# Weights loaded piece by piece into six small tiles, and two output stores of the delta heads issued later

## The chip, the cores and the metric

The kernel runs on one core of one Trainium2 chip. The number that counts is the time of one execution in microseconds of device time, as a median of several runs. Each engine of the core (PE for matrix products, DVE, ACT and POOL for elementwise work, SP as the queue that issues most of the copies) works through its own list of instructions in order, and waits on semaphores for the others. DMA transfers run beside them.

## The reference, cut to what matters

One layer, 256 positions, width 2048, all in float32. A vector `c` gives scale, shift and gate; the normalised input `h` is multiplied by a wide weight matrix, the product is cut into the inputs of two branches, and both are merged and projected back:

```python
shift, scale, gate = jnp.split(jax.nn.silu(c) @ w_ada + b_ada, 3, axis=-1)
h = rms_norm(x, norm_pre_w) * (1.0 + scale[:, None]) + shift[:, None]
proj = h @ w_in                       # 2048 x 24,656 columns, all weights read once
...
o_a = gated_delta_rule(q_a, k_a, v_a, g_log, beta)        # 32 heads, in chunks
o_a = rms_norm(o_a, gdn_norm_w) * jax.nn.silu(gdn_z.astype(jnp.float32)).reshape(...)
y_a = o_a.reshape(b, s, GDN_V_WIDTH).astype(x.dtype) @ w_proj_gdn
...
h_b = mlstm_chunkwise(q_b, k_b, v_b, ml_i + mlstm_b_i, ml_f + mlstm_b_f)   # 8 heads
y_b = h_b.astype(x.dtype) @ w_proj_mlstm
merged = jax.nn.sigmoid(gate_a) * y_a + jax.nn.sigmoid(gate_b) * y_b
out = merged @ w_out
return x + gate[:, None] * rms_norm(out, norm_post_w)
```

Some 320 MB of weights (the copies into `raw` and `ar`) are read, each once, and each weight serves 256 positions.

## The kernel before, in words

**The weight stream.** All weights of the large products go through one object, `Stream`. Its work is a list of *pieces* of 1024 columns by 128 rows (512 KB). For each piece, `prep` makes two tiles out of the raw tile: `whi`, a rounded copy (ACT, L176), and `wlo`, the remainder (DVE, L180; in the first 230 us partly POOL). Then `use` issues the matrix products of the piece: `whi` against the high part of `h`, `wlo` against the high part, `whi` against the low part. There are four `whi` and four `wlo` tiles, so that a piece is prepared up to four pieces before it is used. The raw tiles are loaded by *unit*: a unit is two pieces, one tile of 128 x 2048 (1 MB), and there are three such tiles. The load of a unit is put on SP's list as soon as the last piece of the unit three before it has been prepared in the program (`_loads`, which asks `before["done"]`), and on the chip it waits for that piece's `wlo`.

**What runs beside it.** After each used piece the stream calls `side.step()`, which advances every side generator by one `yield`. These generators hold the delta-rule heads, the mLSTM heads, the convolutions and the merge. `wait(n)` in them means n pieces later. What a generator issues in its step is placed on the engines' lists at this point; on SP it stands behind the loads issued so far. So the order of every engine's list is fixed when the program is built.

**A period.** The delta heads come in eight periods of four heads, from about 320 us to 1000 us. A period has 24 pieces: eight for q and k (`add_proj_t`, names `pt`, L658 and L662), eight for v (`add_proj_n` with a pair of groups, `pn`, L247; each of its loads is two copies, L166, that interleave two groups) and eight for the output gate (`add_z`). The side work of a period that matters here, in its order on SP:

- `ud` (L900): 32 x 32 diagonal blocks of the scores to DRAM, four copies of 16 KB for each of two head pairs; `ug` (L909): four copies that read each block row back to several partitions, 128 KB each; from them DVE computes block inverses (L928 to L934)
- `xd` (L937) and `xcmp` (L941): the inverses to DRAM and back in another layout (four copies); ACT (L948) and DVE (L945, L950) put them into `x0` and `y0`, and PE uses them in `mp`, `mx`, `mq`, `mz` (`gdn_stage2`)
- `vd`, `v`, `cw` (L834, L843, L849): the convolution of v; ACT then applies silu and a scale to `rr` (L885, L889), and PE multiplies it in `pa` (L1039)
- `o_dr` (L1112): the period's finished heads, transposed into two tiles `oT` (L1110), stored to DRAM, 256 KB each; they are read back only by the projection at 1200 us

After the periods come the mLSTM heads (to about 1210 us), the two projections `py` and the output product `pw`. The third part of `w_ada` (the gate) is loaded by the same stream, one unit each, and summed on DVE (L1311, L1313).

Of the kernel before, what the change touches and what calls it, by code (L numbers as in the profile page):

```python
# [15 lines left out]
P = 128  # L16
# [47 lines left out]
class Stream:  # L64


    def __init__(self, load, side, ahead=3):
        self.side, self.ahead = side, ahead
        self.load = (load, "w", 3)
        self.units, self.items, self.rings = [], [], {}  # L70
        self.loaded = self.used = self.prepared = self.pending = 0

    def add(self, src, prep, use, pieces=2, after=None, on_load=None, load=None):
        load, ring, bufs = load or self.load
        r = self.rings.setdefault(ring, [])
        u = dict(src=src, prep=prep, use=use, after=after, on_load=on_load, load=load, done=False,
                 before=r[-bufs] if len(r) >= bufs else None)
        r.append(u)
        i = len(self.units)
        self.units.append(u)  # L80
        for h in range(pieces):
            self.items.append((i, h, h == pieces - 1))

    def _loads(self):

        while self.loaded < len(self.units):
            u = self.units[self.loaded]
            if u["before"] is not None and not u["before"]["done"]:
                return
            u["raw"] = u["load"](u["src"])  # L90
            if u["on_load"]:
                u["on_load"]()
            self.loaded += 1

    def run(self):
        self._loads()
        while self.used < len(self.items):
            while self.prepared < len(self.items) and self.pending <= self.ahead:
                i, h, last = self.items[self.prepared]
                u = self.units[i]  # L100
# [5 lines left out]
            i, h, last = self.items[self.used]  # L106
            u = self.units[i]
            self.used += 1
            if u["use"]:
                self.pending -= 1  # L110
                u["use"](h, *u["p", h])
            if last and u["after"]:
                u["after"]()
            if u["use"]:
                self.side.step()
# [3 lines left out]
def hybrid_layer_kernel(  # L119
# [38 lines left out]
        SP.dma_start(t, src)  # L158
        return t

    def load_w(src):
        raw = wp.tile([P, 2048], F32, name="raw", tag="raw", bufs=3)
        c = 0
        for i, s_ in enumerate(src if isinstance(src, tuple) else (src,)):
            if isinstance(src, tuple) and len(s_.shape) == 3:
                SP.dma_start(raw.rearrange("p (k g c) -> p k g c", k=4, g=2)[:, :, i], s_)  # L166
                continue
            dst = raw[:, c:c + s_.shape[1] * (s_.shape[2] if len(s_.shape) == 3 else 1)]
            c += dst.shape[1]
            if len(s_.shape) == 3:  # L170
                dst = dst.rearrange("p (k n) -> p k n", k=s_.shape[1])
            SP.dma_start(dst, s_)
        return raw

    def split(src, hi, lo, eng=None):
# [29 lines left out]
    def prep_w(h, raw, width=2048):  # L205
# [3 lines left out]
        if begin:  # L209
            begin.pop()(raw[:, 0:n], hi, lo)  # L210
            return hi, lo
        split_w(raw[:, h * 1024:h * 1024 + n], hi[:, 0:n], lo[:, 0:n])
        return hi, lo

    freed = [-1] * 4
# [10 lines left out]
    def gfree(t):  # L226
        freed[slots[1].pop(id(t))[0]] = side.t
# [69 lines left out]
    def ada_tile():  # L297
        return sp.tile([P, 2048], F32, name="ar", tag="ar", bufs=ADA_BUFS)

    def load_ada(src):  # L300
        raw = ada_tile()
        SP.dma_start(raw, src)
        return raw
# [653 lines left out]
    def gdn_stage2(zg, res, zr):  # L957
# [146 lines left out]
        for z in range(2):  # L1104
            for h in range(2):
                for blk in range(2):
                    T.transpose(pts[z][:, h * S + blk * P:h * S + (blk + 1) * P], ons[z][:, blk, h], ident)
        for z in range(2):
            oT = bp.tile([P, 2, S], F32, name="oT", tag="oT")
            A.activation(oT.rearrange("p h t -> p (h t)"), pts[z], AF.Copy, scale=late_c["gnw"][:, 0:1])  # L1110
            gfree(pts[z])
            SP.dma_start(o_dr[4 * zg + 2 * z:4 * zg + 2 * z + 2].rearrange("h d t -> d h t"), oT)  # L1112

    def period_tail(zg, ps, qs, res, zr):
# [182 lines left out]
    def add_gate_unit():  # L1297
# [6 lines left out]
        gate_at[0] += 1  # L1304

        def prep(h, raw):
            side.debt += 2.4
            for q in range(2):
                if i == 0:
                    gate_half.append(bp.tile([P, 1024], F32, name=f"gacc{q}", tag=("ug", "rr")[q], bufs=1 + q))  # L1310
                    V.tensor_scalar(gate_half[q], raw[:, q * 1024:(q + 1) * 1024], sil[:, 0:1], None, op0=ALU.mult)  # L1311
                else:
                    V.scalar_tensor_tensor(gate_half[q], raw[:, q * 1024:(q + 1) * 1024], sil[:, i:i + 1],  # L1313
                                           gate_half[q], op0=ALU.mult, op1=ALU.add)
            if i == KC - 1:
# [318 lines left out]
```

## Time and profile before

| | |
|---|---|
| median of 3 runs | 1574.93 us (1571.59 to 1575.77) |
| the profiled execution | 1578.37 us, of which 1576.6 us lie between its first and last instruction |
| PE busy | 1554.4 us (99%) |
| DVE, ACT, POOL busy | 1172.0, 971.1, 269.9 us |
| DMA | 397.49 MB, mean 252 GB/s, 73.2% of 16 engines' time |
| matrix products | 8256 |
| copies of weights on SP | 227 of 1 MB, 80 of 512 KB, 12 of other sizes |

Busy shares are averages over very different stages. PE is the engine that is nearly always at work, so what counts is when it is not: its idle time, what it waited for then, and the stretches in which its clock is granted at half. A timeline row has the start and the length in us, the engine, the line, the operation, `out<-in`, the shapes, and in square brackets how long the engine was idle before it and what ended that.

### The profile page before, as it was taken

The numbers are of one execution on the slowest core, as the hardware profiler recorded it, in microseconds if no ns is written. First come the engines' busy times: TensorE is split into PE (matmuls) and PEld (weight loads), VectorE is DVE, ScalarE is ACT, GpSimd is POOL, SyncE is SP. The second block draws the span as 40 slices with busy tenths as digits, with TensorE's granted clock in tenths as the row PEclk, the third lists the DMA queues.
The fourth block names the chain that finished last, engine by engine and source line by source line (L and its number), as shares of the span: only waits on it lengthen the run. The fifth ranks groups of instructions, "written<-read, shape, count | busy, mean of one in ns | idle before, by whom it ended". The sixth has DMA issues, their size and how long they took to land.

```text
span 1576.6 us, 22531 instructions
## 1 busy us (share of the span) xinstructions
PE 1554.4 (99%) x8256; PEld 1297.2 (82%) x8256; DVE 1172.0 (74%) x1781; ACT 971.1 (62%) x1638; POOL 269.9 (17%) x213
## 2 busy tenths in 40 slices
PE   8999999999999999999999999999999999999998
PEld 5888888888888888888888888888888888888886
DVE  6786556867798988898979797866768766756654
ACT  7754446767566767676768676666566554544443
POOL 6787761001010101010101010100000000100100
PEclk9999999999999999999999999999999999999999
DMA  9998785975767685868586857656879877766573
GB/s 377 404 386 325 270 294 185 295 242 197 247 221 238 197 263 183 256 193 257 180 246 197 235 194 234 212 200 233 295 260 332 321 270 297 283 238 236 216 270 107
DMA packets 185956, 397.49 MB, mean 252 GB/s; under 512 B 27595, under 2 KB 137825, under 8 KB 158325
## 3 DMA queue, kind: packets, MB, share of 16 engines
q1 hardware_dynamic: 185460, 395.44, 73.2%
q8 instruction: 65, 1.06, 0.3%
q10 hardware_dynamic: 290, 0.53, 0.1%
q14 instruction: 45, 0.37, 0.1%
q0 software_dynamic: 96, 0.09, 0.0%
HBM read 375.37 MB, written 20.64 MB: 251 GB/s over the span
## 4 chain that ended last, share of the span: by engine, by line
PE 61%; issue 14%; DMA 12%; ACT 6%; DVE 5%; POOL 1%; SPq 1%; DVEq 0%; ACTq 0%; POOLq 0%
PE pn L247 37%; PE py L247 8%; PE pt L658 7%; DMA raw<-in_dram 7%; PE pt L662 3%; DMA xcmp<-xd 2%; DVE wlo L180 2%; ACT whi L176 2%; POOL mg L1424 1%; DMA ud<-au 1%; DMA ar<-in_dram 1%; DVE au L816 1%; PE pa L1039 1%; SPq L909 1%; DMA xd<-xx 0%
## 5 line engine op out<-in xcount | busy, mean ns | idle before, releaser
L247 PE MATMUL pn<-whi,h 128*128 128x512 f32 x2304 | 729.1, 392 | 1.0 <-ACT part L493 0.5
L180 DVE TENSOR_TENSOR wlo<-raw,whi 128x1024 fp32r<-128x1024 f32 (+1 forms) x455 | 558.3, 1235 | 210.9 <-ACT whi L176 207.3
L176 ACT CAST whi<-raw 128x1024 fp32r<-128x1024 f32 x508 | 524.1, 1045 | 281.3 <-PE pn L247 155.3
L247 PEld LDWEIGHTS pn<-whi,h 128*128 128x128 f32 x2304 | 432.6, 188 | 91.1 <-ACT h L176 1.1
L247 PE MATMUL pn<-wlo,h 128*128 128x512 f32 x1152 | 448.6, 389 | 0.2 <-POOL wlo L180 0.2
L247 PEld LDWEIGHTS pn<-wlo,h 128*128 128x128 f32 x1152 | 216.5, 188 | 43.4 <-POOL wlo L180 0.8
L658 PE MATMUL pt<-h,whi 128*128 128x512 f32 x768 | 249.6, 407 | 0.0
L247 PE MATMUL py<-whi,y 128*128 128x512 f32 x768 | 239.9, 391 | 0.0
L662 PEld LDWEIGHTS pt<-h,wlo 128*128 128x128 f32 x768 | 146.8, 191 | 34.9
L247 PEld LDWEIGHTS py<-whi,y 128*128 128x128 f32 x768 | 144.2, 188 | 30.3 <-issue 0.6
L180 POOL TENSOR_TENSOR wlo<-raw,whi 128x1024 fp32r<-128x1024 f32 (+1 forms) x67 | 146.5, 2197 | 45.0 <-ACT whi L176 41.3
L662 PE MATMUL pt<-h,wlo 128*128 128x256 f32 x768 | 153.3, 281 | 0.0
L247 PE MATMUL py<-wlo,y 128*128 128x512 f32 x384 | 149.5, 389 | 0.0
L658 PEld LDWEIGHTS pt<-h,whi 128*128 128x128 f32 x768 | 120.3, 192 | 2.4
L747 POOL TENSOR_SCALAR_AFFINE_SELECT dd<-gb 128x256 f32<-128x256 f32 x40 | 36.7, 941 | 451.8 <-DMA gb<-rows 322.6
L176 ACT CAST y<-ya 128x512 fp32r<-128x512 f32 x48 | 29.9, 622 | 129.5 <-PE py L247 119.0
L491 DVE TENSOR_TENSOR part<-pn,part 128x512 f32<-128x512 f32 x112 | 73.7, 685 | 44.9 <-PE pn L247 44.7
L180 DVE TENSOR_TENSOR y<-ya,y 128x512 fp32r<-128x512 f32 x48 | 33.2, 691 | 75.4 <-ACT y L176 75.3
L247 PEld LDWEIGHTS py<-wlo,y 128*128 128x128 f32 x384 | 72.1, 188 | 14.9
L247 PE MATMUL pw<-whi,m 128*128 128x512 f32 x256 | 80.0, 391 | 0.0
L437 DVE SCALAR_TENSOR_TENSOR ar<-ar,csil 128x2048 f32<-128x2048 f32 x30 | 68.3, 2278 | 6.1 <-DMA ar<-in_dram 6.1
L928 DVE TENSOR_TENSOR tmp<-xx,ug 128x6 f32<-128x6 f32 (+15 forms) x128 | 65.4, 511 | 3.2
(272 smaller groups left out, 1475.0 us busy)
## 6 DMA issues: line engine op xcount, KB each, us to landing
raw<-in_dram SPq DMA_DIRECT2D x227, 1024.0 KB
raw<-in_dram SPq DMA_DIRECT2D x80, 512.0 KB
ar<-in_dram SPq DMA_DIRECT2D x31, 1024.0 KB
v<-vd SPq DMA_DIRECT2D x24, 512.0 KB
cw<-conv_dr SPq DMA_DIRECT2D x32, 256.0 KB
ya<-o_dr SPq DMA_DIRECT2D x32, 256.0 KB
gate_dr<-part SPq DMA_DIRECT2D x11, 512.0 KB
gb<-rows SPq DMA_DIRECT2D x20, 256.0 KB
```

Source lines behind the costliest of these rows:

```text
L176: A.copy(hi, src)
L180: eng.tensor_tensor(lo, src, hi.bitcast(F32), op=ALU.subtract)
L247: T.matmul(ps, l, r, start=start and i == 0, stop=stop and i == 2, skip_group_check=True)
L437: V.scalar_tensor_tensor(raw, raw, 1.0, csil, op0=ALU.mult, op1=ALU.mult, accum_out=ad[:, pt * KC + k:pt * KC + k + 1])
L491: V.tensor_tensor(part[g][:, b], ps[b], part[g][:, b], op=ALU.add)
L658: T.matmul(ps, hi[:, o:o + P], h2[:, k].rearrange("p a s -> p (a s)"), start=k == 0, stop=k == KC - 1, skip_group_check=True)
L662: T.matmul(ps[:, 0:S], lo[:, o:o + P], h_hi[:, k], start=False, stop=k == KC - 1, skip_group_check=True)
L747: G.affine_select(dd[:, :, blk * S:blk * S + P], gb[:, :, blk * P:(blk + 1) * P], pattern=[[0, 2], [1, P]], compare_op=ALU.is_ge, fill=-1e ...
L816: V.scalar_tensor_tensor(au[:, h, c0:c0 + 2 * n].rearrange("p (a b) -> p a b", a=2), ps_[:, 0:2 * n].rearrange("p (a b) -> p a b", a=2), c ...
L909: SP.dma_start(ug[32 * q:32 * q + 32], ud[q].rearrange("m j i -> m (j i)").unsqueeze(0).broadcast_to([4, 8, 1024]))
L928: V.tensor_tensor(tmp[:, 0:nq, 0:w, 0:n], xx[:, 0:nq, 0:n].unsqueeze(2).broadcast_to([P, nq, w, n]), ug[:, 0:n, i:i + w].rearrange("p k c ...
L1039: T.matmul(pa[:, c], x0[:, 2 * g], rr[:, 0, c], start=True, stop=True)
```

## The change

A piece, not a unit, becomes what is loaded. The raw tile is 128 x 1024 (512 KB), and there are six instead of three, so that the memory is the same. A load is put on SP's list when the piece six before it has been prepared. The copies of the v pairs become four of 256 KB per pair of pieces in place of two of 512 KB; the gate's units are two pieces now, with the same arithmetic. The lists of PE, DVE, ACT and POOL are the same as before, instruction by instruction; only SP's list differs. It has 942 copies in place of 700.

The second edit: in periods 0 to 6 the two stores of `oT` are issued two and four pieces later, one each, instead of together at once.

```diff
-        self.load = (load, "w", 3)
-        self.units, self.items, self.rings = [], [], {}
+        self.load = (load, "w", 6)
+        self.items, self.rings = [], {}
...
     def add(self, src, prep, use, pieces=2, after=None, on_load=None, load=None):
...
-        u = dict(src=src, prep=prep, use=use, after=after, on_load=on_load, load=load, done=False,
-                 before=r[-bufs] if len(r) >= bufs else None)
...
         for h in range(pieces):
-            self.items.append((i, h, h == pieces - 1))
+            u = dict(src=src, h=h, prep=prep, use=use, after=after if h == pieces - 1 else None,
+                     on_load=on_load if h == 0 else None, load=load, done=False,
+                     before=r[-bufs] if len(r) >= bufs else None)
+            r.append(u)
+            self.items.append(u)
...
-            u["raw"] = u["load"](u["src"])
+            u["raw"] = u["load"](u["src"], u["h"])
...
-                u["p", h] = u["prep"](h, u["raw"])
-                u["done"] = last
+                u["p"] = u["prep"](u["h"], u["raw"])
+                u["done"] = True
...
-    def load_w(src):
-        raw = wp.tile([P, 2048], F32, name="raw", tag="raw", bufs=3)
...
+    def load_w(src, h):
+        raw = wp.tile([P, 1024], F32, name="raw", tag="raw", bufs=6)
+        if not isinstance(src, tuple):
+            if len(src.shape) == 3:
+                k = 1024 // src.shape[2]
+                SP.dma_start(raw.rearrange("p (k n) -> p k n", k=k), src[:, h * k:(h + 1) * k])
+            else:
+                SP.dma_start(raw, src[:, h * 1024:(h + 1) * 1024])
+            return raw
+        if len(src[0].shape) == 3:
+            for i, s_ in enumerate(src):
+                SP.dma_start(raw.rearrange("p (k g c) -> p k g c", k=2, g=2)[:, :, i], s_[:, 2 * h:2 * h + 2])
+            return raw
...
+        oTs = []
         for z in range(2):
             oT = bp.tile([P, 2, S], F32, name="oT", tag="oT")
             A.activation(oT.rearrange("p h t -> p (h t)"), pts[z], AF.Copy, scale=late_c["gnw"][:, 0:1])
             gfree(pts[z])
+            oTs.append(oT)
+        for z, oT in enumerate(oTs):
+            if zg < 7:
+                yield from wait(2)
             SP.dma_start(o_dr[4 * zg + 2 * z:4 * zg + 2 * z + 2].rearrange("h d t -> d h t"), oT)
...
-        stream.add(w_ada[32 + i], prep, None, 1)
+        stream.add(w_ada[32 + i], prep, None)
```

Two places show how SP's list moves; both stand in every full period, and are shown for the same one (about 690 us to 725 us in the profile of before). `raw<-in_dram` is a load of weights; 128x8x256 is a unit of q and k, 128x4x256 from L164 a piece of it (before, the same shape from L166 is one of the two copies of a v unit), 128x2x256 one of the two copies of a v piece.

First, SP from the block stores `ud` to the read-back `xcmp`. Before:

```order
L900 DMA ud<-au 32x4x32 x4
L172 DMA raw<-in_dram 128x8x256
L937 DMA xd<-xx 128x8x32
L172 DMA raw<-in_dram 128x8x256
L843 DMA v_7377<-vd 128x2x512
L849 DMA cw<-conv_dr 128x2x256 x2
L900 DMA ud<-au 32x4x32 x4
L941 DMA xcmp<-xd 32x1x256 x4
```

and with the change:

```order
L906 DMA ud<-au 32x4x32 x4
L164 DMA raw<-in_dram 128x4x256 x3
L943 DMA xd<-xx 128x8x32
L164 DMA raw<-in_dram 128x4x256
L849 DMA v_7655<-vd 128x2x512
L164 DMA raw<-in_dram 128x4x256
L855 DMA cw<-conv_dr 128x2x256 x2
L906 DMA ud<-au 32x4x32 x4
L947 DMA xcmp<-xd 32x1x256 x4
```

Four pieces of q and k stood before `xcmp`, now five do: one more load stands ahead of `xd`, half of the next one behind it, and one more ahead of `cw`.

Second, SP directly behind that, from `xcmp` to the store `vd`. Before:

```order
L941 DMA xcmp<-xd 32x1x256 x4
L172 DMA raw<-in_dram 128x8x256
L1112 DMA o_dr<-oT 128x2x256 x2
L909 DMA ug<-ud 32x1x1024 x4
L172 DMA raw<-in_dram 128x8x256
L166 DMA raw<-in_dram 128x4x256 x4
L834 DMA vd<-rr 128x2x512
```

and with the change:

```order
L947 DMA xcmp<-xd 32x1x256 x4
L164 DMA raw<-in_dram 128x4x256 x2
L915 DMA ug<-ud 32x1x1024 x4
L164 DMA raw<-in_dram 128x4x256
L1123 DMA o_dr<-oT 128x2x256
L170 DMA raw<-in_dram 128x2x256 x4
L1123 DMA o_dr<-oT 128x2x256
L170 DMA raw<-in_dram 128x2x256 x4
L840 DMA vd<-rr 128x2x512
```

Before, pieces 7 and 8 of q and k were one load behind the two stores and the four copies `ug`. Now piece 7 stands ahead of `ug`, only piece 8 behind it, and the stores stand further down among the loads of v.

More of the change, by code (lines that the diff above doesn't have):

```diff
@@ L75, in add @@
         r = self.rings.setdefault(ring, [])
[L76 to L82 removed]
+        for h in range(pieces):
+            u = dict(src=src, h=h, prep=prep, use=use, after=after if h == pieces - 1 else None,
[3 more added lines that the diff above has]
+            self.items.append(u)
     def _loads(self):
[L86 to L87 removed]
+        while self.loaded < len(self.items):
+            u = self.items[self.loaded]
             if u["before"] is not None and not u["before"]["done"]:
                 return
[L90 removed]
+            u["raw"] = u["load"](u["src"], u["h"])
             if u["on_load"]:
@@ L98, in run @@
             while self.prepared < len(self.items) and self.pending <= self.ahead:
-                i, h, last = self.items[self.prepared]
-                u = self.units[i]
+                u = self.items[self.prepared]
                 self.pending += u["use"] is not None
-                u["p", h] = u["prep"](h, u["raw"])
-                u["done"] = last
+                u["p"] = u["prep"](u["h"], u["raw"])
+                u["done"] = True
                 self.prepared += 1
                 self._loads()
-            i, h, last = self.items[self.used]
-            u = self.units[i]
+            u = self.items[self.used]
             self.used += 1
@@ L110, in run @@
                 self.pending -= 1
-                u["use"](h, *u["p", h])
-            if last and u["after"]:
+                u["use"](u["h"], *u["p"])
+            if u["after"]:
                 u["after"]()
@@ L159, in const @@
         return t
-    def load_w(src):
-        raw = wp.tile([P, 2048], F32, name="raw", tag="raw", bufs=3)
[L163 to L172, printed above, removed]
+    def load_w(src, h):
[11 more added lines that the diff above has]
+            return raw
+        c = -h * 1024
+        for s_ in src:
+            n = s_.shape[1]
+            a, b = max(0, -c), min(n, 1024 - c)
+            if a < b:
+                SP.dma_start(raw[:, c + a:c + b], s_[:, a:b])
+            c += n
         return raw
@@ L211, in prep_w @@
             return hi, lo
-        split_w(raw[:, h * 1024:h * 1024 + n], hi[:, 0:n], lo[:, 0:n])
+        split_w(raw[:, 0:n], hi[:, 0:n], lo[:, 0:n])
         return hi, lo
@@ L1306, in prep @@
         def prep(h, raw):
[L1307 to L1315, printed above, removed]
+            side.debt += 1.2
+            if i == 0:
+                gate_half.append(bp.tile([P, 1024], F32, name=f"gacc{h}", tag=("ug", "rr")[h], bufs=1 + h))
+                V.tensor_scalar(gate_half[h], raw, sil[:, 0:1], None, op0=ALU.mult)
+            else:
+                V.scalar_tensor_tensor(gate_half[h], raw, sil[:, i:i + 1], gate_half[h], op0=ALU.mult, op1=ALU.add)
+            if i == KC - 1 and h == 1:
                 side.add(gate_sum())
             return ()
-        stream.add(w_ada[32 + i], prep, None, 1)
+        stream.add(w_ada[32 + i], prep, None)
     def gate_sum():
```

2 lines of the change are left out of this document (1 added, 1 removed).

## The prediction

> **What bounds the kernel now.** First the page's busy times, then what PE waited for, first of 0 to 600 us, then of 600 to 1000 us (columns: total us, times, longest):
>
> ```profile
> PE 1554.4 (99%) x8256; PEld 1297.2 (82%) x8256; DVE 1172.0 (74%) x1781; ACT 971.1 (62%) x1638; POOL 269.9 (17%) x213
> ...
> PE mx L994 <- ACT pcm L983: 1.2, 1, 1.2
> PE pn L247 <- ACT part L493: 0.5, 1, 0.5
> ...
> PE pa L1039 <- ACT rr L889: 5.4, 4, 1.9
> PE mz L1012 <- ACT p L1018: 1.5, 1, 1.5
> PE mx L994 <- ACT pcm L983: 1.0, 2, 0.5
> ```
>
> PE sets the time. The change leaves its list as it is, so it can only act on PE's idle time, 1576.6 - 1554.4 = 22 us in all. Between 600 and 1000 us, where the eight periods' side work runs beside the stream, it is 5.4 + 1.5 + 1.0 = 7.9 us. Small, but each of its long waits has a sequel. The windows right behind four of them, 3.4 us each (columns: window, length, then busy us and instructions of PE, PEld, DVE, ACT, POOL, then the granted clock, DMA share, GB/s), with an ordinary window ahead of them:
>
> ```profile
> 723.30:726.70 3.40, 3.40 (x22) 2.96 (x21) 1.17 (x3) 1.91 (x4) 0.00 (x0) 1.00 0.85 267
> 730.00:733.40 3.40, 3.40 (x13) 2.83 (x12) 3.29 (x9) 3.40 (x7) 0.00 (x0) 0.51 0.57 186
> 811.90:815.30 3.40, 3.40 (x13) 3.01 (x14) 3.26 (x10) 3.35 (x6) 0.00 (x0) 0.50 0.68 220
> 893.80:897.20 3.40, 3.40 (x12) 2.84 (x12) 3.18 (x10) 2.77 (x5) 0.00 (x0) 0.50 0.83 269
> 972.30:975.70 3.40, 3.40 (x13) 2.92 (x12) 3.19 (x11) 3.38 (x9) 0.00 (x0) 0.50 0.20 78
> ```
>
> The clock is at half and PE does 13 products where it did 22; busy time hides it. Each such window loses 3.4 x 0.5 = 1.7 us.
>
> Who is late? ACT's list around the first of these waits, and PE's:
>
> ```profile
> 718.27 0.78 ACT L1018 ACTIVATE p<-mq 64x256 f32<-64x256 f32 x2 [1.47 <-PE mq L1012]
> 724.76 1.05 ACT L176 CAST whi<-raw 128x1024 fp32r<-128x1024 f32 x1 [5.71 <-DMA raw<-in_dram]
> 725.72 0.76 ACT L1025 COPY x<-mz 64x256 f32<-64x256 f32 x2
> ...
> 721.17 0.68 PE L1012 MATMUL mz<-x,p 64*64 64x64 f32 x16
> 727.24 0.39 PE L662 MATMUL pt<-h,wlo 128*128 128x256 f32 x2
> 729.51 1.80 PE L1039 MATMUL pa<-rr,x 128*128 128x128 f32 x7 [1.88 <-ACT rr L889]
> ```
>
> PE waits for `rr`, which ACT has ready late because a weight cast stood ahead of it in ACT's list and waited 5.71 us for its load. And SP, which issued that load:
>
> ```profile
> 702.37 3.81 SPq L941 DMA_DIRECT2D xcmp<-xd  x4
> 706.27 0.40 SPq L172 DMA_DIRECT2D raw<-in_dram  x1
> 706.77 1.03 SPq L1112 DMA_DIRECT2D o_dr<-oT  x2
> 707.86 2.71 SPq L909 DMA_DIRECT2D ug<-ud  x4
> 710.67 0.42 SPq L172 DMA_DIRECT2D raw<-in_dram  x1
> ...
> 697.15 5.20 DMA raw<-in_dram
> 710.67 14.02 DMA raw<-in_dram
> ```
>
> The last two rows are from the chain of waits. A unit issued at 697.15 us took 5.2 us; the unit issued at 710.67, behind two stores and the four `ug`, took 14.0 us (to 724.7). It holds pieces 7 and 8 of q and k, and ACT's late cast is piece 7. The DMA rows agree that the queue is clogged just then and empty elsewhere:
>
> ```profile
> 695.00:698.00 3.00, 3.00 (x15) 2.50 (x14) 2.90 (x11) 1.06 (x1) 0.70 (x1) 1.00 0.02 2
> 713.00:720.00 7.00, 7.00 (x97) 5.95 (x96) 5.97 (x7) 4.43 (x11) 0.00 (x0) 1.00 1.10 233
> 732.00:735.00 3.00, 3.00 (x15) 2.56 (x15) 2.79 (x8) 1.89 (x4) 0.00 (x0) 0.77 1.05 353
> ```
>
> While `ug` is under way all engines are taken (1.10) but move 233 GB/s; loads alone move 353.
>
> **Part 1, the loads by piece.** Both orders of SP's list stand ahead of this. Piece 7 leaves the place behind `ug` and stands ahead of it. `xcmp` ends at 706.2 us (702.37 + 3.81); two loads at 0.4 us follow, so piece 7 is issued by 707.0, and at a unit's 5.2 us it is there by 712. ACT asks for it at 719.05 (end of `p`). The 5.71 us wait goes, with 7 us to spare.
>
> Then piece 8 is late next: issued behind `ug` at 707.0 + 2.7 = 709.8 us. Its landing has two bounds: 14.0 us as before, 723.8; or less what no longer stands ahead of it or belongs to it, half a MB of stores and half a MB of itself, 1 MB at 353 GB/s = 3.0 us, 720.8. When is it needed? An undisturbed period shows the distance (the first row, of the chain, gives PE's time for a product: 195.94 / 864 = 0.227 us, so 2.72 us for a piece of 12):
>
> ```profile
> 56.69 195.94 PE pn L247 x864
> ...
> 565.01 0.76 ACT L1025 COPY x<-mz 64x256 f32<-64x256 f32 x2 [0.23 <-PE mz L1012]
> 567.29 1.06 ACT L176 CAST whi<-raw 128x1024 fp32r<-128x1024 f32 x1
> 568.24 1.72 ACT L889 ACTIVATE rr<-rr,sk 128x256 f32<-128x256 f32 x4
> 570.60 0.60 PE L1039 MATMUL pa<-rr,x 128*128 128x128 f32 x4
> ```
>
> Its cast begins 2.3 us behind the copy that follows `mz`, and `rr` is ready 0.6 us before PE takes it. With `mz` at 721.17 the copy starts at 721.9, so the cast is due at 724.2, later than both bounds. PE does not wait at `pa`. The same list stands in the other periods; once the late cast stands ahead of `p`, and PE waits at `mz` instead. Gain: 5.4 + 1.5 = **6.9 us** at most; I take all of it, as both bounds allow. If no stall of this kind is left, the half clock goes too: 4 x 1.7 = **6.8 us**.
>
> On that second term the Trainium skill ("TensorE: Matmul & The Clock Gate", "HAM oscillation") gives a rule that speaks against it: only idle gaps of more than about 3.4 us bring the clock down. Waits of 1.5 to 1.9 us would then be harmless, and the gain 6.9 us alone. The rows above differ: each half-clock window begins right at such a wait. By the page the time would be that of the second rival below.
>
> **Part 2, what SP pays.** 242 more copies, at 0.40 us (a `raw` above) to 0.95 us (an `xcmp`, 3.81 / 4) are 97 to 230 us of SP, spread over 1576. SP computes nothing; it costs only where something urgent stands behind. That is `xd` to `xcmp`, whose read-back ACT awaits (waits of ACT and of SP, 600 to 1000 us; the last three rows are from the lists of ACT, PE and DVE):
>
> ```profile
> ACT whi L176 <- DMA raw<-in_dram: 27.6, 5, 6.9
> ACT x L948 <- DMA xcmp<-xd: 16.2, 6, 3.7
> ...
> SPq L941 <- DMA v<-vd: 3.4, 5, 0.7
> SPq L941 <- DMA cw<-conv_dr: 1.2, 3, 0.6
> ...
> 712.57 1.06 ACT L983 COPY pcm<-mp 32x128 f32<-32x128 f32 x4
> 714.02 0.21 PE L994 MATMUL mx<-xcmp,pcm 32*32 32x32 f32 x1
> 722.17 0.09 DVE L915 MEMSET ug<- 128x32 f32 x1 [2.05 <-DMA ug<-ud]
> ```
>
> `xcmp` reads neither `v` nor `cw`, yet its issue waits for their landing: the program gives each copy of SP one of eight landing semaphores in turn, so a copy waits until the eighth before it has landed. The new list puts one more half load ahead of `cw`, but the bytes between 697 and `xcmp` stay at 2 MB (half a MB leaves ahead of 697, where the queue is empty). So `cw` lands at the same time, to within the 0.4 + 0.4 us that SP needs for the added copies. `mx` on PE follows `pcm`'s end, 713.63, at 714.02, so 0.4 us are to spare. Bounds: 0, and (0.8 - 0.4) x 5 periods = 2 us. I take **+1 us**, between ends that lie close. (What a whole piece time would cost is the third rival.)
>
> **Part 3, edits at nothing.** The stores moved: their reader is 200 us and more away; 1.03 us of SP and 0.5 MB leave `ug`'s front and stand among the loads of v, the first of which is due a piece behind piece 8, at 727; without that slack the same 1 to 1.5 us a period would show. Smaller rows in DRAM (4 KB for 8 KB) concern stages in which PE waits for no load; what they cost uncovered is the fourth rival. The start, where DMA is full: SP's sequence there is the same, loads can only be earlier; PE's waits of 0.5 + 0.3 us bound a gain, and I count none. The 1.2 us at `mx` near 490 us stay: there `xcmp` stands behind `ug` in both lists.
>
> **Sum.** -6.9 - 6.8 + 1 = -12.7 us against the profiled execution's 1578.37 us: 1565.7. The median shown is 1574.93, 3.4 us lower, a little more than two half-clock windows, so timed runs may have fewer of these. I subtract the sum from the median: **1562 us** (0.8% less). Its own range: down to 1556 (the 1 us is not paid, the waits at `mx`, 1.2 + 1.0 us, go as well, and 2 us for the spread of the runs) and up to 1568 (PE loses 1.2 us in each of five periods again).
>
> **Rivals.**
>
> 1. *Slower: the eight semaphores.* With loads half as large, eight copies in flight are half the bytes. Behind `ug` come piece 8, a store, then v loads as two copies a piece: the third of these, piece 10, needs `ug`'s first landing, the next ones the others'. If `ug` lands at 722 as now (the DVE row above) and a load issued then takes 14 us like the one behind `ug`, piece 10 comes at 736; it is due two pieces behind piece 8, at 724.2 + 2 x 2.7 = 729.6. That wait of 6.4 us is worse than today's 5.71, and it holds up `vd` behind it in SP's list, so that PE waits a second time a period: 1575 + 1 + 5 x (0.7 + 1.9) = 1589. For it: `ug` is slow and holds four of eight. Against: nothing slow is queued by then, and at 5.2 us piece 10 lands at 727. It decides from 7.4 us of landing time on. Chance 0.13.
> 2. *The clock falls for another reason.* The waits go, the half clock stays: 1575 - 6.9 + 1 = 1569. Against: all four stand at a wait. Chance 0.08.
> 3. *No change: the wait moves to `mx`.* `xd` does stand behind one more load, whose slot comes a piece later. If all of a piece's 2.7 us reached `xcmp`, `mx` would wait 2.7 - 0.4 = 2.3 us a period: 1575 - 13.7 + 5 x 2.3 = 1573, and 1.7 us more for each of these that brings the clock down. Against: `xd` waits for a slot when DMA moves 2 GB/s, so what follows catches up. Chance 0.15.
> 4. *Smaller copies are slower copies.* If halves ran at half the rate, 177 GB/s, 512 KB would take 2.97 us against a piece's 2.72, and PE would starve: 0.25 us for two pieces of each of 227 units, 114 us, 1689. The Trainium skill ("DMA: Bandwidth & Descriptors", "Measured (HBM→SBUF, 128 partitions, SWDGE, issued from GpSimd)") does advise at least 1 MiB a transfer for three quarters of the peak. The trace does not bear it out for copies that overlap: the window at 732 us is made of 512 KB copies of v and `vd`'s read-back, and moves 353. Chance 0.01.
>
> **Chances and range.** Forecast 0.63. What a measurement of this kernel can tell from no change is 0.3%, 4.7 us. Faster: forecast and rival 2, 0.71. Within it: rival 3, 0.15. Slower: rivals 1 and 4, 0.14. The range must reach beyond the forecast's own upper end to rivals 2 and 3: 1556 to 1576 leaves out most of 0.14 above and a little below.
>
> **What would show it.** In the changed profile: the ACT wait for `raw` between 600 and 1000 us, now 27.6 us in five waits, under 8; no PE wait at `pa` and none of over 1 us; the granted clock at 1.00 between 17 and 1570 us; piece 7's load issued ahead of `ug`. The waits of ACT for `xcmp` (16.2 us in six) should stay within 5 us of that. Wrong: waits of ACT or DVE for loads of v, or `mx` waits of 2 us.

## The result, and the profile after

The changed kernel takes 1561.61 us (median of 5 runs, 1560.51 to 1563.16), the kernel before 1574.93 (5 runs, 1571.59 to 1576.74): a ratio of 0.9921, 95% interval 0.9907 to 0.9934. The forecast was 1562. The profiled execution took 1561.96 us with a span of 1560.2, which is 16.4 us less than the span before.

The page's busy times, and PE's waits over the whole span down to half a microsecond (columns: total us, times, longest):

```profile
PE 1545.2 (99%) x8256; PEld 1291.3 (83%) x8256; DVE 1171.8 (75%) x1781; ACT 972.5 (62%) x1638; POOL 267.6 (17%) x213
...
PE csil L325 <- ACT ar L323: 3.9, 1, 3.9
PE mx L1000 <- ACT pcm L989: 1.5, 1, 1.5
PE mp L984 <- DVE ycmp L951: 0.9, 1, 0.9
PE pn L253 <- DVE part L501: 0.5, 1, 0.5
```

None of these lies between 600 and 1000 us: the waits at `pa`, `mz` and `mx` there, 7.9 us before, are gone. Nor does ACT wait for `raw` there any more (27.6 us before). Two of the four windows that ran at half clock before, in the changed kernel:

```profile
730.00:733.40 3.40, 3.40 (x24) 3.04 (x23) 3.33 (x8) 1.43 (x3) 0.00 (x0) 1.00 0.85 252
811.90:815.30 3.40, 3.40 (x16) 2.77 (x16) 3.36 (x8) 1.62 (x4) 0.00 (x0) 1.00 0.84 242
```

Where the time went can be read from two marks on PE, the first product of q and k (`pt`) and the first of the projections (`py`). Timeline rows of the kernel before, then of the changed one:

```profile
335.13 0.62 PE L658 MATMUL pt<-h,whi 128*128 128x512 f32 x2
...
1210.78 0.48 PE L247 MATMUL py<-whi,y 128*128 128x512 f32 x1
```

```profile
334.26 0.61 PE L664 MATMUL pt<-h,whi 128*128 128x512 f32 x2
...
1194.40 0.48 PE L253 MATMUL py<-whi,y 128*128 128x512 f32 x1
```

From mark to mark it was 875.65 us and is 860.14, 15.5 us less; ahead of it 0.9 us were gained (a second profile of the changed kernel, experiment 12, has this mark at 334.8 us, so most of that is chance), behind it nothing. The 15.5 are 7.9 us of listed waits and 4 x 1.7 = 6.8 us of half clock, less 1.2 us that the waits near 490 us grew by (2.4 for 1.2), and 2.0 us that neither list shows. These 2.0 are hardly idle time: PE's idle time between the marks fell from 9.3 to 2.5 us, by 6.8, of which 6.7 are the listed waits (7.9 - 1.2). Product by product, the four places with a half-clock window (near 730, 811, 893 and 971 us) became 14.9 us shorter, where waits and half clock make 13.3; so some 0.4 us at each of them lies in longer products beside the wait, and why they are longer is not shown.

SP's list around the place that the prediction speaks of, ACT's behind it, and what SP itself waited for between 600 and 1000 us:

```profile
702.03 3.19 SPq L947 DMA_DIRECT2D xcmp<-xd  x4
705.32 0.95 SPq L164 DMA_DIRECT2D raw<-in_dram  x2
706.32 2.61 SPq L915 DMA_DIRECT2D ug<-ud  x4
709.03 0.40 SPq L164 DMA_DIRECT2D raw<-in_dram  x1
709.47 0.67 SPq L1123 DMA_DIRECT2D o_dr<-oT  x1
```

```profile
718.09 1.05 ACT L182 CAST whi<-raw 128x1024 fp32r<-128x1024 f32 x1
720.89 0.76 ACT L1031 COPY x<-mz 64x256 f32<-64x256 f32 x2 [1.75 <-PE mz L1018]
...
723.17 1.07 ACT L182 CAST whi<-raw 128x1024 fp32r<-128x1024 f32 x1
724.13 1.71 ACT L895 ACTIVATE rr<-rr,sk 128x256 f32<-128x256 f32 x4
```

```profile
SPq L170 <- DMA ug<-ud: 6.4, 7, 1.7
```

Piece 7 is issued ahead of `ug` and its cast (718.09) waits for nothing; piece 8, behind `ug`, is cast at 723.17 without a wait either. SP does wait for `ug`'s landings, as the first rival said (on other lines too, 14.4 us in 14 waits together), but never over 1.7 us, and neither ACT nor DVE waits more than 0.5 us for a load of weights there. So far this shows what happened, not which of the two edits did it, nor why the load was late.

### The profile page after: what moved, and what is told of

The parts are those of the page before. It is cut to its first block, busy times and chain, and to the rows that moved or that the text cites. A ratio compares the mean times of both kernels' runs of the same rounds, so it can differ in the third digit from the quotient of the medians.

```text
span 1560.2 us, 23408 instructions
## 1 busy us (share of the span) xinstructions
PE 1545.2 (99%) x8256; PEld 1291.3 (83%) x8256; DVE 1171.8 (75%) x1781; ACT 972.5 (62%) x1638; POOL 267.6 (17%) x213
## 3 DMA queue, kind: packets, MB, share of 16 engines
q1 hardware_dynamic: 213892, 395.46, 77.5%
## 4 chain that ended last, share of the span: by engine, by line
PE 78%; issue 13%; DMA 3%; DVE 3%; ACT 1%; POOL 1%; SPq 0%; DVEq 0%; POOLq 0%; ACTq 0%
PE pn L253 47%; PE pt L664 10%; PE py L253 8%; PE pt L668 5%; DMA raw<-in_dram 1%; DVE wlo L186 1%; DMA xcmp<-xd 1%; PE psa L253 1%; ACT whi L182 1%; PE csil L325 0%; DMA gs<-gate_dr 0%; PE po L1073 0%; PE po L1074 0%; PE po L1071 0%; PE pb L1053 0%
## 5 line engine op out<-in xcount | busy, mean ns | idle before, releaser
L664 PE MATMUL pt<-h,whi 128*128 128x512 f32 x768 | 245.6, 401 | 0.0
L253 PEld LDWEIGHTS py<-wlo,y 128*128 128x128 f32 x384 | 72.1, 188 | 14.9
```

What stands on the lines that cost most here:

```text
L253: T.matmul(ps, l, r, start=start and i == 0, stop=stop and i == 2, skip_group_check=True)
L664: T.matmul(ps, hi[:, o:o + P], h2[:, k].rearrange("p a s -> p (a s)"), start=k == 0, stop=k == KC - 1, skip_group_check=True)
```

## The experiments

**1 and 2: each edit alone.** In the first the loads are as before and the stores are moved; in the second the reverse.

```diff
 # experiment 1, on the kernel before
+        oTs = []
         for z in range(2):
             oT = bp.tile([P, 2, S], F32, name="oT", tag="oT")
 ...
-            SP.dma_start(o_dr[...], oT)
+            oTs.append(oT)
+        for z, oT in enumerate(oTs):
+            if zg < 7:
+                yield from wait(2)
+            SP.dma_start(o_dr[...], oT)
```

> The kernel before with only the stores of the finished heads moved (two and four pieces later); loads by unit of 1 MB, three tiles. The theory (the cast of piece 7 is late because its load stands behind ug and the stores): the unit of pieces 7 and 8 stays behind ug, but half a MB leaves its front, 1.4 us at 353 GB/s to 2.2 us at 233. ACT's five waits for raw (27.6 us between 600 and 1000 us) fall to 3.5 to 4.3 us each, PE's waits at pa (1.9, 1.7, 1.5) to under 0.5, and with them the half clock behind them goes: 1563 to 1570 us. The rival (only the loads by piece matter, the stores are off the path): no change, 1573 to 1576, and the four half-clock windows stay.

> The changed kernel with the two stores put back where they were, together and at once; loads by piece in six tiles. The theory: piece 7 is ahead of ug, so ACT does not wait for it and PE does not wait at pa; piece 8 lands 1.4 to 2.2 us later than in the changed kernel, which is hidden or costs ACT a wait of under 2 us: 1560 to 1566 us, clock 1.00 throughout. The rival (the moved stores carry the gain): PE waits at pa and the half clock are back, 1568 to 1575.

Measured: the stores alone 1562.09 us (0.993, 0.991 to 0.9949), the loads alone 1561.38 (0.9928, 0.9908 to 0.9948). The first is just under the 1563 to 1570 us expected, the second inside its range. Each edit gives the whole gain as far as these runs can tell, and both together give no more. Neither has a listed PE wait at `pa` or `mz`, nor a half-clock window there. The waits of ACT for `raw`, 600 to 1000 us, and SP's list, with the stores alone:

```profile
ACT whi L176 <- DMA raw<-in_dram: 15.1, 5, 4.2
```

```profile
703.49 0.40 SPq L172 DMA_DIRECT2D raw<-in_dram  x1
703.93 2.60 SPq L909 DMA_DIRECT2D ug<-ud  x4
706.63 0.40 SPq L172 DMA_DIRECT2D raw<-in_dram  x1
707.07 3.33 SPq L1117 DMA_DIRECT2D o_dr<-oT  x1
```

The unit with pieces 7 and 8 still stands behind `ug`, and ACT still waits five times, but 3.0 us each in place of 5.5. That is the 1.4 to 2.2 us for half a MB and a little more, and it is enough: `rr` is then ready before PE asks for it. With the loads alone ACT's wait is one of 0.6 us. The rivals of both expectations fall.

**3: place or size?** The kernel before, loads whole, stores in place, but `ug` one piece later:

```diff
         ug = bp.tile([P, 32, 32], F32, name="ug", tag="ug", bufs=1)
+        yield from wait(1)
         for q in range(4):
             SP.dma_start(ug[32 * q:32 * q + 32], ...)
-        yield from wait(5)
+        yield from wait(4)
```

> The kernel before, loads by unit of 1 MB and the stores where they were, but ug is issued one piece later (and its use as late as before), so that the unit of pieces 7 and 8 stands ahead of ug. The theory (the place behind ug decides, not the size of a load): ACT's waits for raw in 600 to 1000 us fall from 27.6 to under 8 us, no PE wait at pa, no half clock there; ug lands up to 2.7 us later, which costs DVE a longer wait at its first use and may put 0 to 1 us a period on PE: 1560 to 1568 us. The rival (it is the halved load with a landing of its own that helps): no change, 1572 to 1577.

Measured: 1571.0 us (0.9995, 0.9982 to 1.0008), so no gain in the time, outside the 1560 to 1568 of the theory. But the waits say more than the sum does. PE's, ACT's and DVE's waits between 600 and 1000 us:

```profile
PE mx L995 <- ACT pcm L984: 2.0, 2, 1.1
PE psa L247 <- DVE ql L777: 1.6, 4, 0.4
PE pn L247 <- DVE wlo L180: 1.6, 2, 0.9
```

```profile
ACT whi L176 <- DMA raw<-in_dram: 1.5, 2, 1.0
...
DVE nsu L918 <- DMA ug<-ud: 18.1, 4, 5.1
```

ACT's waits for the load are gone with whole 1 MB units, as are the waits at `pa` and the half clock: the place behind `ug` was the cause of the late load. What came in their place is DVE, which now stands 18.1 us in four waits for `ug` (2.8 in three and 2.1 in one before), and PE then waits for `wlo` and `ql`, which stand behind it on DVE's list. The expectation put 0 to 1 us a period on that price, and it was more: the span of 1568.3 us is 10 us above that of experiment 1, and 9 of these 10 arise between 675 and 985 us.

**4: half loads in the old order.** The changed kernel, but a unit's two loads are issued only when both tiles are free:

```diff
             if u["before"] is not None and not u["before"]["done"]:
                 return
+            if u["h"] == 0 and self.loaded + 1 < len(self.items):
+                v = self.items[self.loaded + 1]
+                if v["src"] is u["src"] and v["before"] is not None and not v["before"]["done"]:
+                    return
```

> The changed kernel (half loads in six tiles, stores moved), but the two loads of a unit are issued together once both tiles are free: pieces 7 and 8 both stand behind ug again, as before. The theory (place): piece 7 has lost half a MB of stores and half a MB of its own unit from its front against before, 1.4 to 2.2 us each, so ACT's wait for it is 5.7 - 2.8 to 5.7 - 4.4, 1.3 to 2.9 us, in four or five periods; PE's slack at pa covers that, so the time is within 3 us of the changed kernel, 1558 to 1565, with those ACT waits back. The rival (size: a landing of its own suffices): ACT's waits for raw stay at 0, as in the changed kernel.

Measured: 1559.56 us (0.9915, 0.9892 to 0.9937). ACT's waits for `raw` are back in five places:

```profile
ACT whi L186 <- DMA raw<-in_dram: 4.7, 5, 2.2
```

They are 0.9 us on average, the longest inside the 1.3 to 2.9 us expected, the average below it: standing behind `ug` still costs, though less than I had worked out, and PE does not feel it. That a piece has a landing of its own helps too, then. The Trainium skill ("Perfetto Trace Analysis", "DMA Optimizations") says that splitting a transfer may let some of the work start sooner; this row against experiment 1's (15.1 us in five) agrees with it.

**5: the clock.** Eight products that nobody uses fill PE's wait ahead of `pa` in three periods; the fourth wait stays as a control.

```diff
         pa = gtile("pa", True)
+        for _ in range(8 if zg in FILL else 0):
+            T.matmul(pa, h_hi[:, 0, 0:P], h2[:, 1].rearrange("p a s -> p (a s)"), start=True, stop=True)
```

> The kernel before with eight extra products (128x128 by 512 columns, their results overwritten) in PE's list right ahead of pa in the periods whose pa waits 1.9, 1.7 and 1.5 us; at 0.227 us each, 1.8 us, they fill those waits. The fourth wait of this kind (at mz near 970 us) is left as a control. The theory (the idle time of PE brings the clock down): the three half-clock windows behind pa go, the one near 972 us stays; the products cost 0 to 0.4 us each time, so the execution is 4 to 5 us shorter than one of the kernel before with all four windows (span 1576.6, clock 0.995): span 1571 to 1573. The rival (the clock falls for another reason): windows of 0.5 behind all four, span 1576 to 1578. A run of the kernel before that has no such window would be 6.8 us shorter than its profiled one, by the theory: among its timed runs the mean granted clock should go with the time.

Measured: 1574.57 us (1.0008, 0.9996 to 1.0021); the profiled span is 1575.3 us, not 1571 to 1573. Windows behind the first filled wait, and at and behind the control:

```profile
730.40:733.80 3.40, 3.40 (x21) 3.05 (x22) 3.26 (x10) 3.40 (x7) 0.00 (x0) 1.00 0.67 219
...
965.70:969.10 3.40, 1.66 (x20) 1.36 (x21) 2.01 (x6) 3.16 (x6) 0.00 (x0) 1.00 0.50 197
969.10:972.50 3.40, 3.40 (x13) 2.92 (x12) 3.19 (x11) 3.38 (x9) 0.00 (x0) 0.51 0.16 60
```

The three windows are gone, the fourth is there: PE's idle time brings the clock down, in one execution with its own control. Product by product, the three filled places are some 4 us shorter together, as expected. Why the span falls by 1.3 us alone is in PE's waits of 600 to 1300 us:

```profile
PE mz L1013 <- ACT p L1019: 2.4, 1, 2.4
PE py L248 <- ACT vt L1238: 1.6, 1, 1.6
PE pa L1042 <- ACT rr L890: 1.3, 3, 0.7
```

The control was 0.9 us longer in this execution (2.4 for 1.5) and a wait of 1.6 us came at `py`, which the kernel before does not have; the products from there on are 1.9 us later. Where that wait comes from is open. And filling is no saving: the products take as long as the wait, and in an execution whose clock would not have fallen they gain nothing.

That the number of half-clock windows differs from run to run shows in the timed runs of the kernel before. There are 49 of them, on the four chips on which the experiments ran, and the mean granted clock of each goes with its time:

| mean clock | runs | mean us |
|---|---|---|
| 0.999 | 8 | 1570.1 |
| 0.998 | 14 | 1571.9 |
| 0.997 | 15 | 1573.5 |
| 0.996 | 6 | 1574.8 |
| 0.995 | 5 | 1576.5 |

One more run had 0.994 and 1580.6 us. A window of 3.4 us at half is 0.001 of the span's mean clock, and each 0.001 costs 1.6 us here, near the 1.7 of the prediction. The profiled execution before (0.995) had four such windows. The changed kernel shows 0.998 to 0.999 in all runs, and the profiles at these values have no such window up to the last product; so runs of the kernel before at 0.999 had none, and the median run of the 49 (0.997) had one or two. It took 1572.9 us, 2.8 us more than the mean at 0.999.

**6: does `ug` hold up the load?** Its four copies stay in place and number but carry a sixteenth of the bytes.

```diff
-            SP.dma_start(ug[32 * q:32 * q + 32],
-                         ud[q].rearrange("m j i -> m (j i)").unsqueeze(0).broadcast_to([4, 8, 1024]))
+            SP.dma_start(ug[32 * q:32 * q + 32].rearrange("p j i -> p (j i)")[:, 0:64],
+                         ud[q].rearrange("m j i -> m (j i)")[:, 0:64].unsqueeze(0).broadcast_to([4, 8, 64]))
+        G.memset(ug.rearrange("p j i -> p (j i)")[:, 64:1024], 0.0)
```

> The kernel before, with each of the four ug copies reading only 64 of its 1024 columns (32 KB of 512 KB in all; the rest of ug is set to zero by POOL, so the block inverses are not computed from the real scores and the output is not the reference's); number, order and place of all copies stay. The theory (the slow ug copies hold up the loads behind them): ACT's waits for raw in 600 to 1000 us fall from 27.6 to under 5 us, no PE wait at pa, no half clock: span 1558 to 1564. The rival (ug's bytes do not matter: the late load is late for SP's issue, the stores, or its own size): waits of 3 to 6 us stay, span 1568 to 1577.

Measured: span 1558.9 us (one run, 1560.67), no wait of ACT for `raw` between 600 and 1000 us, no half-clock window, and one wait of PE:

```profile
PE mx L995 <- DMA ug<-ud: 0.7, 1, 0.7
```

With a sixteenth of the bytes and the same four issues on SP the late load is gone: `ug`'s bytes, not its issues, are what held the unit up. Half a MB of `ug` has packets under way for 8.5 us in the kernel before (712.6 to 721.1); half a MB at the 353 GB/s of loads alone would take an estimated 1.5.

**7: how long must PE idle?** 18 gaps of chosen length in PE's list where it otherwise never waits.

```diff
+                    for i in range(2):
+                        T.matmul(st_["ps"][3][:, 0:P], late["z"][:, 0:P], hi[:, 0:P], start=False, stop=False,
+                                 skip_group_check=True)
+                        while i == 0 and n > 0:
+                            c = late["z"][:, 0:min(n, 1024)]
+                            G.tensor_scalar(c, c.bitcast(F32), 1.0, None, op0=ALU.mult)
+                            n -= 1024
```

> The changed kernel with 18 idle gaps put into PE's list between 1200 and 1480 us, where it otherwise never waits: PE multiplies by a tile of zeros (added to the running sums, which stay as they are), POOL rewrites the tile (64 to 3584 columns, so that PE waits some 0.3 to 5 us), PE multiplies by it again. The theory of the prediction: an idle gap of under 1.2 us leaves the granted clock at 1.00, gaps of 1.5 us and more are followed by a window of 3.4 us at 0.5 (1.7 us lost each, beside the gap itself), as behind the four waits of the kernel before. The rival, by the rule that the prediction weighed against this (the Trainium skill, TensorE: Matmul & The Clock Gate, HAM oscillation): no window at 0.5 behind any gap under about 3.4 us, so at most behind the one or two longest.

Four of the gaps (PE rows, the idle time in brackets), and the clock behind the second, third and fourth:

```profile
1296.64 0.33 PE L1398 MATMUL py<-whi,z 128*128 128x128 f32 x1 [1.52 <-POOL z L1402]
...
1317.44 0.33 PE L1398 MATMUL py<-whi,z 128*128 128x128 f32 x1 [2.47 <-POOL z L1402]
...
1329.69 0.33 PE L1398 MATMUL py<-whi,z 128*128 128x128 f32 x1 [2.02 <-POOL z L1402]
...
1481.61 0.33 PE L1398 MATMUL py<-whi,z 128*128 128x128 f32 x1 [1.99 <-POOL z L1402]
```

```profile
1318.30:1321.70 3.40, 3.40 (x9) 2.65 (x9) 0.00 (x0) 0.00 (x0) 0.00 (x0) 0.50 0.68 236
1331.90:1335.30 3.40, 3.40 (x17) 2.81 (x16) 0.46 (x1) 0.00 (x0) 0.00 (x0) 1.00 0.98 320
1482.10:1485.50 3.40, 3.40 (x10) 2.63 (x9) 0.00 (x0) 0.00 (x0) 0.00 (x0) 0.50 0.85 288
```

It took 1662.21 us (one run), of which the gaps are 67. POOL was slower than planned, so the longest gap was 11.2 us and not 5. Gaps of 2.47 and 1.99 us were followed by a window at half clock, the gap of 2.02 us shown was not, nor were the two of 1.5, for which the theory had asked. What tells the 1.99 from the 2.02 is where they lie: all half-clock windows of an execution start on one grid of 3.413 us. The gap of 1.99 us lies in one cell of it (1478.7 to 1482.1), the one of 2.02 is cut by an edge at 1328.5 into 0.8 and 1.2. Counted over the profiles of this study, and without the last 30 us of each, cells at full clock in which PE idled 1.7 us (half a cell) to 3.2 us were followed by half clock 18 times of 18; of six with 1.52 to 1.58 us two were, and none with less. The bound that the expectation drew from the waits of the kernel before, between 1.2 and 1.5 us, was near, but it holds for the idle time in a cell and not for the length of a gap. The rule of the Trainium skill ("TensorE: Matmul & The Clock Gate", "HAM oscillation") that only gaps over about 3.4 us matter differs from these rows, which decide: five gaps of 2.0 to 3.0 us in this run alone brought the clock down.

**8: the first period.** PE's waits near 485 to 490 us, where the first period's `xcmp` stands behind the second's `ug`:

```diff
-FIRST_ROOM_US = 3.2
+FIRST_ROOM_US = 6.0
```

> The changed kernel with one constant changed (FIRST_ROOM_US 3.2 to 6.0, the share of a piece time that the first period's block inverse may take on DVE): xd of the first period is issued five pieces' places earlier and its xcmp stands ahead of the second period's ug, as in all later periods. The theory (a copy behind ug is late): PE's waits at mp and mx near 485 to 490 us (0.9 + 1.5 us) go, and nothing else changes: 1 to 2.5 us less than the changed kernel, 1559 to 1561 us. The rival: DVE's inverse steps, now more at a time, make wlo late between 390 and 460 us, and PE waits there 1 us or more instead: 1561 to 1564.

Measured: 1563.13 us (0.9923, 0.9903 to 0.9944). That is no gain, and inside the rival's range, but its runs (1561.92 to 1565.14) overlap those of the changed kernel (1560.51 to 1565.48, on other chips), so the waits have to decide. Waits of PE, 320 to 1000 us:

```profile
PE mx L1000 <- ACT pcm L989: 2.5, 3, 1.5
PE psa L253 <- DVE ql L783: 0.8, 1, 0.8
PE pn L253 <- DVE wlo L186: 0.5, 1, 0.5
```

The waits for `wlo` and `ql` lie at 450 to 454 us, 1.3 us together, as the rival said: DVE paid for the new order. A wait of 0.8 us at `mx` is left near 480, and one of 1.5 us came near 559, which neither side had named.

**9 and 10: `ug` in one copy.** A way to get rid of `ug`'s weight, on the kernel before and on the changed one:

```diff
-        for q in range(4):
-            SP.dma_start(ug[32 * q:32 * q + 32],
-                         ud[q].rearrange("m j i -> m (j i)").unsqueeze(0).broadcast_to([4, 8, 1024]))
+        SP.dma_start(ug.rearrange("p j i -> p (j i)"),
+                     ud.rearrange("q m j i -> (q m) (j i)").unsqueeze(0).broadcast_to([4, 32, 1024]))
...
-        SP.dma_start(xd.rearrange("qq q rg m i -> (q rg m) qq i"), xx)
+        SP.dma_start(xd.rearrange("qq rg q m i -> (rg q m) qq i"), xx)
...
-            SP.dma_start(xcmp[32 * q:32 * q + 32], xd[:, q])
+            SP.dma_start(xcmp[32 * q:32 * q + 32], xd[:, :, q])
```

> The kernel before (loads by unit, stores at once), with ug read back by one copy of 128 rows of 4 KB in place of four of 32 rows; for that the order of ug's partitions changes (repeat, block, head in place of block, repeat, head), with the matching constant and the layout of xd. The bytes and the place stay. The trace of the kernel before shows the four copies at 16 packets of 4 KB a microsecond, 0.25 us each, for 8 us: about four of 16 DMA engines busy with them, the 1 KB packets of the loads meanwhile at 150 a microsecond against 250 to 360. The theory (each of the four copies sits on one engine, and the loads' share on these four engines is late): a copy of 128 rows spreads over more engines, 128 packets x 0.25 / 16 = 2 us, so the load behind it lands some 5 us earlier; ACT's waits for raw in 600 to 1000 us fall from 27.6 to under 5 us, no PE wait at pa and no half clock: 1558 to 1564 us. The rival (32 rows to an engine whatever the copy, or the order of issue alone): the packets still come at 16 a microsecond over 8 us, the waits stay, 1570 to 1576.

> The same edit of ug on the changed kernel: SP issues 3 copies fewer a period (about 2 us of 2.6), and ug is read in one copy. The theory: the middle has no PE wait left to remove, so the gain is only what remains near 480 to 490 us, 0 to 3 us: 1558 to 1562. The rival (more engines busy with ug now delay the read-back of xcmp or the loads elsewhere): PE waits of 1 us or more at mx, 1562 to 1566.

Measured: 1595.83 us on the kernel before (1.014, 1.0115 to 1.0166) and 1566.42 on the changed one (0.9955, 0.9938 to 0.9973). The theory fell in both. On the changed kernel PE waited 2.0 us at `mp` near 487 us, with a half-clock window behind, and 2.4 us in four at `mx`; the rival had looked for such waits at `mx`, and for a little less time. On the kernel before it became worse than with four copies. Of that run, PE's and ACT's waits of 600 to 1000 us, SP's list, and the load in the chain of waits:

```profile
PE pa L1038 <- ACT rr L889: 13.0, 4, 3.7
PE mz L1011 <- ACT p L1017: 4.7, 1, 4.7
...
ACT whi L176 <- DMA raw<-in_dram: 38.8, 5, 10.4
```

```profile
716.05 0.55 SPq L908 DMA_DIRECT2D ug<-ud  x1
716.70 0.66 SPq L172 DMA_DIRECT2D raw<-in_dram  x1
...
716.70 17.46 DMA raw<-in_dram
```

In the trace's packets one copy moves as the four did: 128 packets of 4 KB, mostly 13 to 16 a microsecond at 0.27 us each, from 720.8 to 730.2 us. Their times add up to about 4 of 16 DMA engines at work. The load behind it lands at 734.2, 3.7 us after `ug`'s last packet has ended (730.4); before it was 724.7, 3.6 us after 721.1. In both the load follows the end of `ug`. The Trainium skill ("DMA: Bandwidth & Descriptors", "Why a DMA increments its semaphore by 16 and not by 1") has a rule for the number of engines: the largest number up to 16 that divides the slowest dimension of both sides of a copy, and these are the lowest-numbered engines. For all these copies the slowest dimension of the source is the broadcast, of 4, so the rule gives 4. The packet counts agree, with four copies and with one; which engines they were, no run here shows. Nor does this alone explain the late load: while `ug` is under way the loads' packets of 1 KB are slow nearly all, not one in four (in the kernel before, between 714 and 719 us, 99% of them took over 0.06 us, 0.085 in the median; between 709 and 712 us the median was 0.046). How `ug` slows the others stays open. A copy whose slowest dimension is a multiple of 16 was not tried.

**11 and 12: the paired loads against the change.** Experiment 4 once more and the changed kernel once more, side by side.

> The kernel of the paired loads once more, side by side with the changed kernel, since its median was the lowest of all (1559.56 us). If pairs are better (fewer places where SP waits between copies, so that xcmp of the first period is read back earlier): PE's waits at mp and mx near 485 to 490 us stay under 1.5 us in sum and the median is 1558 to 1561, 1 us or more below the changed kernel's. If it was chance: both medians within 1 us of each other, 1560 to 1562.

> The changed kernel itself, with a second profile. PE's loss near 485 to 490 us was 4.3 us of excess in its first profile and 2.4 with the stores put back, though the list is the same there: if that is chance, the second profile shows 2 to 3 us and a span near 1558 to 1560; if it belongs to the change, 4 us again. Median 1560 to 1563, granted clock 0.998 or more in all runs, as no wait in the middle is long enough to bring it down, and a spread of under 4 us where the kernel before has 7 to 9.

Measured: pairs 1559.55 us (1559.38 to 1560.65; 0.991, 0.9886 to 0.9933), the changed kernel 1562.29 (1561.13 to 1565.48; 0.9928, 0.9908 to 0.9947). The two ranges do not overlap, so the pairs are the fastest version here, by 2.7 us. Between 320 and 1000 us PE has no listed wait in the first; in the changed kernel, with ACT's waits for `xcmp` of the changed kernel and of the pairs (320 to 1000 us):

```profile
PE mx L1000 <- ACT pcm L989: 1.1, 2, 0.6
...
ACT x L954 <- DMA xcmp<-xd: 20.5, 9, 5.0
```

```profile
ACT x L958 <- DMA xcmp<-xd: 12.8, 10, 3.8
```

The order of the pairs leaves `xcmp` the place it had before, while loads by piece put half a MB more ahead of `cw` and so of `xcmp`. That this is why the pairs are faster is not shown: the same kernel waited 17.1 us for `xcmp` in its profile of experiment 4, the kernel before 21.9, and PE's waits explain 1.1 of the 2.7 us. The waits at 485 to 490 us, 2.4 us in the first profile of the change, are one of 0.5 in the second, so they differ from execution to execution. The spread of the changed kernel was 4.4 us, more than the 4 expected; its granted clock was 0.998 or 0.999 in all runs, as expected.

## Why the prediction was right, and where it was not

**What bounds the kernel: right.** The late cast of piece 7, behind `ug` and the stores, made PE wait, and the waits brought the clock down. Experiments 1, 3 and 6 each shorten or remove the wait for the late load in another way (what stands ahead of `ug`, `ug`'s place, `ug`'s bytes), and each time the waits at `pa` and the half clock go with it.

**Term 1, the stall, -6.9 us: right, a little small.** In the profile the listed waits in the middle fell by 7.9 us, and another 2.0 went in products beside the waits, which the prediction did not count. In the timed runs it can be had without the clock: runs of the kernel before at 0.999 take 1570.1 us, the change 1561.6 to 1562.3, so 8 us.

**Term 2, the half clock, -6.8 us: right for the profiled execution, wrong for the median.** The prediction had seen that the median lay 3.4 us lower, "so timed runs may have fewer of these", and then took all four windows off that median all the same. The median run has one or two, 2.8 us (1572.9 less 1570.1). By its own remark it should have said 1574.9 - 6.9 - 3.4 + 1 = 1565.6; that it came out at 1562 is partly luck. 4 us too many for the clock (6.8 for 2.8) stood against 2 us too few for the stall (8 for 5.9, with the third term) and a first median 2 us above that of the 49 runs (1572.9): 1572.9 - 8 - 2.8 = 1562.1 is the sum that the runs show.

**Term 3, what SP pays, +1 us: not settled.** The list has 997 copies, not 942 (476 loads of 512 KB and 140 of 256 KB in place of 319, beside 381 others), so 297 more than before, not 242: 119 to 282 us of SP at the prediction's prices. That changes nothing in its argument, which goes by who stands behind a copy. In the first profile `mx` had no wait between 600 and 1000 us, in the second one of 0.6. Against the pairs, the order by piece costs 2.7 us of median, over the upper bound of 2; but the stores alone, which add no copy, are no faster than the change (1562.09 us), so no run gives SP's price by itself.

**Part 3, the stores at nothing: wrong.** "The stores moved: their reader is 200 us and more away" is true and looks at the wrong side. What counts of a copy in a queue is also who stands behind it. The half MB was in the prediction's own bounds for piece 8 (3.0 us for 1 MB), and the same figure for the unit behind `ug`, with the 233 GB/s under `ug` as the slower end, would have shown that the stores alone take 1.4 to 2.2 us off a wait of 5.7, of which PE felt only 1.9. Experiment 1 shows that this suffices: the prediction credited one edit with a gain that either gives.

**The rivals.** The eight semaphores: SP's waits for `ug`'s landing came, at most 1.7 us each, and nothing starved. The clock falling for another reason: refuted by experiment 5. The wait moving to `mx`: not in the first profile between 600 and 1000 us, and a small part of it in the second (one `mx` wait of 0.6 us near 634 us). Smaller copies slower: between 713 and 720 us, the stretch that moved 233 GB/s before,

```profile
713.00:720.00 7.00, 7.00 (x97) 6.02 (x96) 6.10 (x13) 4.44 (x9) 0.00 (x0) 1.00 1.07 278
```

it moves 278 now. That is no clean comparison, as `ug`'s packets end at 716.8 us here and at 721.1 before. Over the whole execution the smaller copies do cost something: SP's queue took 77.5% of 16 engines' time against 73.2% for the same 395 MB, 5% more packet time in all. No engine waits for it between 600 and 1000 us, beyond the 0.5 us named above.

**The marks that the prediction named** came but for one: ACT's wait for `raw` at 0 (under 8 was asked), no wait at `pa`, the clock at 1.00 from 17 us to the last product, piece 7 ahead of `ug`, ACT's waits for `xcmp` at 15.3 us (16.2 before). A PE wait of 1.5 us at 489 us broke "none of over 1 us"; in the second profile of the same kernel it is 0.5.

## What to carry to other kernels

Look for the one slow transfer in a queue, then at everything that stands ahead of a load that is due soon: moving any of it away, the load or the ballast, may give the same gain, and the gains do not add up. When a profile shows windows at a lower clock, check from the timed runs' mean clocks how many the median run has before taking them off a median. A transfer that is moved later frees those behind it and makes its own reader wait, so price both sides.

## What the runs showed of the hardware

PE's clock is judged on a fixed grid of 3.413 us (experiment 7): a cell at full clock in which it idled 1.7 us or more was followed by one at half clock 18 times of 18, cells of 1.52 to 1.58 us were two times of six, cells with less never; a gap of 2.0 us passed unpunished because a cell's edge cut it. A broadcast copy of half a MB had packets under way for 8 to 10 us, as much as about 4 of 16 DMA engines would carry, whether it was issued as four copies or as one. A load of 1 MB behind it took 14.0 to 17.5 us where another took 5.2.
